# Twelve of twenty-two pairs per half by seven products in the down projection, with some activation sums kept, and fast pairs later in the gate's first half

## The chip, the cores and the metric

One Trainium2 chip, one of its cores. The metric is the device time in microseconds (us) of one execution of the whole program, as the median of three runs. A profile is one further execution, recorded instruction by instruction.

## The reference

One encoder layer on 256 tokens of width 2048, in float32. Cut to the parts that matter here (the mixer ahead of them yields `h`):

```python
hn = rmsnorm(h, ffn_norm_pre)
up = hn @ w_ffn_up                        # 2048 -> 2 x 5632
gate, val = split(up, 2)
gate = dwconv_centred(gate, ffn_conv_w, ffn_conv_b)
ff = (gelu(gate) * val) @ w_ffn_down      # "down": 5632 -> 2048
h = h + rmsnorm(ff, ffn_norm_post)
g = sigmoid(rmsnorm(h, ple_norm_pre) @ w_ple_gate)      # "gate": 2048 -> 2048
h = h + rmsnorm(g * (p @ w_ple), ple_norm_post)         # "PLE"
```

## The kernel before

**Precision and cost of a product.** Every float32 operand of a large product is split into a high and a low part of a type that TensorE reads at full speed (`split`, from line 139): ScalarE copies the high part (L150), VectorE subtracts it from the original for the low part (L151). A product is then three matmuls: high by high, high by low, low by high.

**Token-major products** (`token_major`, from line 289) compute down and gate. The output is 256 tokens by 2048 columns. It is made in two halves of 1024 columns; a half keeps four accumulators of 128 tokens by 512 columns in PSUM. The contraction runs in units `u` of two blocks of 128 (`k`, `k+1`): 22 units per half of down (5632 = 44 x 128), 8 per half of the gate. The order of the blocks comes from a list `ks`. A unit is done in one of two ways:

- *classic*: one load of 1 MB (`raw`, three buffers), two splits of 128 x 1024, 24 matmuls;
- *fast* (`seven_products`, when `u` is in the list `fast`): the unit is a product of two by two blocks (two token halves, two k blocks, two column halves) and is formed with seven block products instead of eight, 21 matmuls. It needs sums of weight blocks and sums of activation blocks. Four splits are made: `a` (128 x 512) and `b` (128 x 1024) of raw weight blocks (loads of 256 and 512 KB), `c` and `d` (128 x 1024) of the block sums `t` (1 MB). The products' order is: three matmuls with `a`, six with `b`, six with `c`, six with `d`. Some products go to extra accumulators `alt`, and `combine` adds them at the end of the half with VectorE.

**Sums of weight blocks** (`block_sums`) are formed ahead of time, during the up projection. Each is a fetch of two weight blocks into a page, three additions on VectorE, and a store to DRAM, put as jobs into a list `work` with 88 slots, of which `feature_pairs` runs one after each of its rounds; sum `i` uses the slots 3i+2 to 3i+5. The list `which` holds the pairs in order of use; its first two are formed last and stay in their pages, with no store. All others are loaded back when their unit needs them (`dns`, `gts` in the profile are the DRAM copies, `dn012t` is the load for half 0, k=12; as output of a matmul, `dns`, `dn0s`, `gts` and `gt0s` are the accumulators `alt`).

**Sums of activation blocks.** In down `hid_sums` (line 898) forms them from the page of activations at each fast unit, in both halves anew: four VectorE instructions of 128 x 128 into a `mid` tile `hd` (L757 to L760 in `pair_sums`), a ScalarE copy (L761) and a VectorE subtraction (L762) of 128 x 512 into a `mid` tile `he`. In the gate the class `Sums` does the same, with the result in half a page (`psp`), and keeps it: the second half finds the pairs of the first in `got`. `get_hid` splits the activations of a unit (`hs`, L883 and L884).

**Memory and order.** There are 13 pages of 128 x 2048 for large tiles (six hold the activations `hid` during down, others the output `dnm`, the residual `hb`, block sums, panels), three `mid` tiles, three raw buffers, five split buffers of each kind. Loads go out in order on one queue (SP). The framework places waits and orders each engine's instructions at build time; the program sets the priorities by its order. At unit 13 of down's second half the residual is loaded back (`back`), at unit 16 the gate's first pair is loaded and split ahead (`first_gate`: `gtf`, `gtfh`, `gtfl`).

After down, `panel_part` transposes the normalised result into the gate's stationary operand (`dnx`), PLE's product is formed, `row_rstd` squares the rows (junk in pages `rpj`), and the gate's two halves follow.

The lists that the change touches are on lines 845 and 846:

```python
dn_fast, gt_fast = ((2, 4, 6, 8, 9, 11, 13, 14, 16, 18, 19), (1, 3, 5, 7, 8, 10, 12, 14, 16, 17, 19)), ((2, 4, 6), (1, 2))
gt_ks = list(range(NK)), [0, 1, 4, 5, 8, 9, 2, 3, 6, 7, 10, 11, 12, 13, 14, 15]
```

Of the kernel before, what the change touches and what calls it, by code (L numbers as in the profile page):

```python
# [12 lines left out]
F32R = mybir.dt.float32r  # L13
# [3 lines left out]
P = 128  # L17
L = 256
D = 2048
NK = D // P  # L20
# [31 lines left out]
def build(nc, a, out):  # L52
# [5 lines left out]
    with tile.TileContext(nc) as tc, \  # L58
# [12 lines left out]
        def page(name, dtype=F32):  # L71
            return gp.tile([P, 2048], dtype, tag="pg", bufs=13, name=name)

        def mid(name, dtype=F32):
            return gp.tile([P, 1024], dtype, tag="mid", bufs=3, name=name)
# [365 lines left out]
        for u in range(0, NK, 2):  # L441
            r = [wp.tile([P, 2048], F32, tag="raw", bufs=3, name=f"dtur{u}") if u else r0, page(f"dtur{u + 1}")]
            for j in range(2):
                k = u + j
# [17 lines left out]
            for j in range(2):  # L462
                k = u + j
# [290 lines left out]
        def pair_sums(name, s, o, a11, a21, a12, a22):  # L754

            s1, s2, s3, s4 = (s[:, i * P:(i + 1) * P] for i in range(4))
            nc.vector.tensor_sub(s1, a22, a21)  # L757
            nc.vector.tensor_sub(s3, a11, a21)
            nc.vector.tensor_add(s2, s1, a11)
            nc.vector.tensor_sub(s4, a12, s2)  # L760
            nc.scalar.copy(o[:, :512], s[:, :512])  # L761
            nc.vector.tensor_sub(o[:, 512:], s[:, :512], o[:, :512].bitcast(F32))  # L762
            return {f"s{i + 1}": (o[:, i * P:(i + 1) * P], o[:, 512 + i * P:512 + (i + 1) * P]) for i in range(4)}
# [78 lines left out]
            h_kept.append(dp.tile([P, D], F32, tag=f"h{t}", bufs=1, name=f"h_kept{t}"))  # L842
            load(h_kept[t], h[t])

        dn_fast, gt_fast = ((2, 4, 6, 8, 9, 11, 13, 14, 16, 18, 19), (1, 3, 5, 7, 8, 10, 12, 14, 16, 17, 19)), ((2, 4, 6), (1, 2))
        gt_ks = list(range(NK)), [0, 1, 4, 5, 8, 9, 2, 3, 6, 7, 10, 11, 12, 13, 14, 15]
        which = [("dn", w_down, c * 1024, 2 * u) for c in range(2) for u in dn_fast[c]] + \
            [("gt", w_gate, c * 1024, gt_ks[c][2 * u]) for c in range(2) for u in gt_fast[c]]
        work.extend([] for _ in range(8 * DFF // 512))
# [3 lines left out]
        hid = []  # L853
        for s in range(DFF // 512):
            sc = mid(f"gr{s}")
            for i in range(2):
                ga = main(f"ga{s}{i}")
                feature_pairs(f"ug{s}{i}", w_up, s * 512 + i * 256, hf, ga)
                o = sc[:, i * 512:(i + 1) * 512]
# [7 lines left out]
            for i in range(2):  # L867
# [5 lines left out]
                hd = hid[s // 2][:, c0:c0 + 512]  # L873
# [5 lines left out]
        def get_hid(k):  # L879
            if k % 2 == 0:  # L880
                t = lp.tile([P, 1024], F32R, tag="hs", bufs=2, name=f"hs{k}")
                src = hid[k // 8][:, (k % 8) * L:(k % 8 + 2) * L]
                nc.scalar.copy(t[:, :512], src)  # L883
                nc.vector.tensor_sub(t[:, 512:], src, t[:, :512].bitcast(F32))  # L884
                cur["t"] = t
            o = (k % 2) * L
            return cur["t"][:, o:o + L], cur["t"][:, 512 + o:512 + o + L]
# [3 lines left out]
        def hid_get(k):  # L891
# [3 lines left out]
                hcache[k0], hcache[k0 + 1] = get_hid(k0), get_hid(k0 + 1)  # L895
            return hcache[k]

        def hid_sums(k):

            (h1, l1), (h2, l2) = get_hid(k), get_hid(k + 1)  # L900
            src = hid[k // 8][:, (k % 8) * L:(k % 8 + 2) * L]
            d = pair_sums(f"hd{k}", mid(f"hd{k}"), mid(f"he{k}", F32R), *(src[:, i * P:(i + 1) * P] for i in range(4)))
            return dict(d, a11=(h1[:, :P], l1[:, :P]), a12=(h2[:, :P], l2[:, :P]), a22=(h2[:, P:], l2[:, P:]))

        def back():
# [5 lines left out]
        def first_gate():  # L911
# [7 lines left out]
            for j in range(2):  # L919
                ready[f"gt00_{j}"] = hi[:, j * 1024:(j + 1) * 1024], lo[:, j * 1024:(j + 1) * 1024]  # L920

        hp = sublayer("dn", w_down, list(range(NF)), hid_get, gload("gffn", a["ffn_norm_post"][0]), h, V_PN,
                      fast=dn_fast, sums=hid_sums, at={13: back, 16: first_gate})


# [114 lines left out]
```

## Time and profile before

| | us |
|---|---|
| median of three runs | 1142.09 (1141.17 to 1142.82) |
| the profiled execution, its own time | 1140.26 |
| its span, first to last instruction | 1138.5 |
| TensorE busy | 1115.9 (98%) |
| VectorE busy | 935.8 (82%) |
| ScalarE busy | 637.6 (56%) |
| mean granted TensorE clock | 0.995 |

In the profile PE is TensorE's matmuls and PEld its weight loads, DVE is VectorE, ACT ScalarE, POOL GpSimd, SP the engine whose queue issues the DMAs. L87 is line 87 of the kernel. A row of a timeline gives start and duration in us, engine, line, operation, output and inputs by the program's names, shapes, and in brackets the idle time of the engine just before and what ended it. Matmuls overlap: a duration of 0.39 us goes with a start every 0.23 us, so starts are compared. A row of the table by stage gives the stage, its length, then for each engine the busy time and the number of instructions, then the granted clock, the share of time that the DMA engines were busy and their rate. A row of waits gives who waited for whom: us in total, times, the longest. A row of a DMA issue ends with KB and the us from issue to landing.

### The profile page before, as it was taken

The numbers are of one execution on the slowest core, as the hardware profiler recorded it, in microseconds if no ns is written. First come the engines' busy times: TensorE is split into PE (matmuls) and PEld (weight loads), VectorE is DVE, ScalarE is ACT, GpSimd is POOL, SyncE is SP. The second block draws the span as 40 slices with busy tenths as digits, with TensorE's granted clock in tenths as the row PEclk, the third lists the DMA queues.
The fourth block names the chain that finished last, engine by engine and source line by source line (L and its number), as shares of the span: only waits on it lengthen the run. The fifth ranks groups of instructions, "written<-read, shape, count | busy, mean of one in ns | idle before, by whom it ended". The sixth has DMA issues, their size and how long they took to land.

```text
span 1138.5 us, 15770 instructions
## 1 busy us (share of the span) xinstructions
PE 1115.9 (98%) x5982; PEld 962.5 (85%) x5982; DVE 935.8 (82%) x1277; ACT 637.6 (56%) x869; POOL 128.9 (11%) x124
## 2 busy tenths in 40 slices
PE   9998999999999999999999999999999999998996
PEld 9997987888888888888888888888888888886775
DVE  6579896699888877877877778867799999998795
ACT  7533543555674554544545545545677777776672
POOL 0274504200110100000000000000000000102001
PEclk9999999999999999999999999999999999999999
DMA  9952347545699999998999898966985589985673
GB/s 359 341 184 75 112 151 263 200 164 187 240 311 332 328 325 313 320 294 299 333 335 313 291 323 309 323 218 223 352 286 184 176 301 344 343 277 193 203 236 107
DMA packets 145419, 297.97 MB, mean 262 GB/s; under 512 B 5440, under 2 KB 98496, under 8 KB 137536
## 3 DMA queue, kind: packets, MB, share of 16 engines
q1 hardware_dynamic: 144784, 295.56, 76.4%
q0 software_dynamic: 272, 1.05, 0.5%
q8 instruction: 47, 0.77, 0.3%
q10 hardware_dynamic: 288, 0.36, 0.1%
q14 instruction: 28, 0.23, 0.1%
HBM read 266.54 MB, written 30.41 MB: 261 GB/s over the span
## 4 chain that ended last, share of the span: by engine, by line
PE 91%; DVE 5%; ACT 1%; DMA 1%; POOL 1%; issue 1%; DVEq 0%; POOLq 0%; ACTq 0%
PE va L87 22%; PE ga L87 21%; PE dna L87 15%; PE woa L87 7%; PE gt L87 4%; PE dtu L87 4%; PE z L87 4%; PE xbc L87 3%; PE dns L87 3%; DVE cv L426 2%; PE dn0s L87 1%; PE dn1s L87 1%; PE ple L87 1%; DMA gt04t<-gts 1%; DVE w L639 1%
## 5 line engine op out<-in xcount | busy, mean ns | idle before, releaser
L87 PE MATMUL ga<-wox,ug_0h 128*128 128x512 f32 x352 | 125.6, 395 | 0.0
L87 PE MATMUL ga<-wox,ug_1h 128*128 128x512 f32 x352 | 125.1, 394 | 0.0
L87 PE MATMUL va<-wox,uv_1h 128*128 128x512 f32 x352 | 124.8, 394 | 0.0
L87 PE MATMUL va<-wox,uv_0h 128*128 128x512 f32 x352 | 124.8, 394 | 0.0
L87 PE MATMUL ga<-wox,ug_1l 128*128 128x256 f32 x352 | 99.3, 282 | 0.0
L87 PE MATMUL ga<-wox,ug_0l 128*128 128x256 f32 x352 | 99.3, 282 | 0.0
L87 PE MATMUL va<-wox,uv_1l 128*128 128x256 f32 x352 | 99.2, 282 | 0.0
L87 PE MATMUL va<-wox,uv_0l 128*128 128x256 f32 x352 | 99.2, 282 | 0.0
L87 PEld LDWEIGHTS va<-wox,uv_1h 128*128 128x128 f32 x352 | 66.2, 188 | 14.8
L87 PEld LDWEIGHTS va<-wox,uv_0h 128*128 128x128 f32 x352 | 66.2, 188 | 14.8
L87 PEld LDWEIGHTS ga<-wox,ug_0h 128*128 128x128 f32 x352 | 66.2, 188 | 14.7
L87 PEld LDWEIGHTS ga<-wox,ug_1h 128*128 128x128 f32 x352 | 66.2, 188 | 14.7
L865 POOL TENSOR_TENSOR fc<-fc,rfb 128x1024 f32<-128x1024 f32 x11 | 28.0, 2546 | 438.6 <-ACT fc L864 438.6
L87 PEld LDWEIGHTS ga<-wox,ug_0l 128*128 128x128 f32 x352 | 66.3, 188 | 0.1
L87 PEld LDWEIGHTS ga<-wox,ug_1l 128*128 128x128 f32 x352 | 66.3, 188 | 0.0
L87 PEld LDWEIGHTS va<-wox,uv_0l 128*128 128x128 f32 x352 | 66.3, 188 | 0.0
L87 PEld LDWEIGHTS va<-wox,uv_1l 128*128 128x128 f32 x352 | 66.3, 188 | 0.0
L87 PE MATMUL dna<-dn_0h,hs 128*128 128x512 f32 x176 | 54.8, 394 | 0.0
L87 PE MATMUL dna<-dn_1h,hs 128*128 128x512 f32 x176 | 54.6, 393 | 0.0
L233 DVE TENSOR_TENSOR dnb<-dnb 128x1024 f32<-128x1024 f32 x22 | 28.0, 1271 | 16.1 <-DMA dnb<-w_ffn_down 16.1
L87 PEld LDWEIGHTS dna<-dn_1h,hs 128*128 128x128 f32 x176 | 33.1, 188 | 7.7
L87 PEld LDWEIGHTS dna<-dn_0h,hs 128*128 128x128 f32 x176 | 33.0, 188 | 7.6
(1866 smaller groups left out, 3136.0 us busy)
## 6 DMA issues: line engine op xcount, KB each, us to landing
dnb<-w_ffn_down SPq DMA_DIRECT2D x22, 1024.0 KB, 10.2
dns<-dnb SPq DMA_DIRECT2D x20, 1024.0 KB, 7.3
dn0r<-w_ffn_down SPq DMA_DIRECT2D x11, 1024.0 KB, 5.8
dn1r<-w_ffn_down SPq DMA_DIRECT2D x11, 1024.0 KB, 7.4
zr<-w_in SPq DMA_DIRECT2D x8, 1024.0 KB, 5.1
dtur<-w_in SPq DMA_DIRECT2D x14, 528.0 KB, 8.8
wo0r<-w_out SPq DMA_DIRECT2D x7, 1024.0 KB, 5.5
wo1r<-w_out SPq DMA_DIRECT2D x6, 1024.0 KB, 5.7
```

Of the source, the lines that this page charges most:

```text
L87: nc.tensor.matmul(o, lhsT, rhs, start=start, stop=stop, skip_group_check=True)
L233: nc.vector.tensor_add(v[:, 0:2], v[:, 0:2], v[:, 1::2])
L426: nc.vector.scalar_tensor_tensor(o[:, lo:hi], i[:, lo + d:hi + d], vec(wcol + j * wstep + f), o[:, lo:hi], op0=ALU.mult, op1=ALU.add)
L639: nc.vector.scalar_tensor_tensor(w[:, h * P:(h + 1) * P], cbm[:, 0, g, t, :], dt[:, t, 8 * g + h:8 * g + h + 1], w[:, h * P:(h + 1) * P], ...
L865: nc.gpsimd.tensor_tensor(cv.rearrange("p (f t) -> p f t", f=4), cv.rearrange("p (f t) -> p f t", f=4), rfb.unsqueeze(1).to_broadcast([P, ...
```

## The change

Three lists and one function are changed:

- down's fast units become 2, 3, 5, 7, 8, 10, 12, 13, 15, 16, 18, 19 in both halves: twelve instead of eleven, and the same ones in both;
- the activation sums of units 3, 8, 13 and 18 (k = 6, 16, 26, 36) are written by the first half not into a `mid` tile but into half a page each (two pages, `hsum6` and `hsum26`), kept, and used again by the second half without forming them;
- the gate's first half has fast units 4 and 6 (k = 8, 12) instead of 2, 4 and 6 (k = 4, 8, 12). Its second half keeps fast units 1 and 2, and its order of blocks is changed so that these are k = 12 and 8 instead of 4 and 8, whose activation sums the first half has formed. 28 sums of weight blocks are formed in place of 27; the two that stay in pages are those of down's units 2 and 3 instead of 2 and 4.

```diff
-        dn_fast, gt_fast = ((2, 4, 6, 8, 9, 11, 13, 14, 16, 18, 19), (1, 3, 5, 7, 8, 10, 12, 14, 16, 17, 19)), ((2, 4, 6), (1, 2))
-        gt_ks = list(range(NK)), [0, 1, 4, 5, 8, 9, 2, 3, 6, 7, 10, 11, 12, 13, 14, 15]
+        dn_fast, gt_fast, dn_keep = ((2, 3, 5, 7, 8, 10, 12, 13, 15, 16, 18, 19), (2, 3, 5, 7, 8, 10, 12, 13, 15, 16, 18, 19)), ((4, 6), (1, 2)), (3, 8, 13, 18)
+        gt_ks = list(range(NK)), [0, 1, 12, 13, 8, 9, 2, 3, 4, 5, 6, 7, 10, 11, 14, 15]
...
+        keep, kept = [], {}
+
         def hid_sums(k):

             (h1, l1), (h2, l2) = get_hid(k), get_hid(k + 1)
-            src = hid[k // 8][:, (k % 8) * L:(k % 8 + 2) * L]
-            d = pair_sums(f"hd{k}", mid(f"hd{k}"), mid(f"he{k}", F32R), *(src[:, i * P:(i + 1) * P] for i in range(4)))
+            if k not in kept:
+                src = hid[k // 8][:, (k % 8) * L:(k % 8 + 2) * L]
+                n = dn_keep.index(k // 2) if k // 2 in dn_keep else -1
+                if n >= 0 and n % 2 == 0:
+                    keep.append(page(f"hsum{k}", F32R))
+                o = keep[-1][:, n % 2 * 1024:(n % 2 + 1) * 1024] if n >= 0 else mid(f"he{k}", F32R)
+                d = pair_sums(f"hd{k}", mid(f"hd{k}"), o, *(src[:, i * P:(i + 1) * P] for i in range(4)))
+                if n >= 0:
+                    kept[k] = d
+            else:
+                d = kept[k]
             return dict(d, a11=(h1[:, :P], l1[:, :P]), a12=(h2[:, :P], l2[:, :P]), a22=(h2[:, P:], l2[:, P:]))
```

## The prediction

> **What bounds the kernel now.** I read the table of busy time by stage first, then the list of what TensorE waited for, then the chain of waits, and last the single instructions around the one long wait. The stages are: up projection to 798 us, first half of down to 912, second half to 1027, then PLE and gate.
>
> ```profile
> core 0: us, PE busy (x) PEld busy (x) DVE busy (x) ACT busy (x) POOL busy (x), PEclk, DMA share, GB/s
> 302.00:798.00 496.00, 495.45 (x2848) 435.45 (x2847) 396.19 (x509) 257.30 (x345) 29.48 (x15) 1.00 0.92 304
> 798.00:912.00 114.00, 114.00 (x496) 92.79 (x495) 102.64 (x144) 79.29 (x106) 0.00 (x0) 1.00 0.72 246
> 912.00:1027.00 115.00, 115.00 (x500) 93.50 (x499) 107.82 (x156) 85.12 (x110) 4.87 (x7) 1.00 0.90 313
> 1027.00:1060.00 33.00, 28.26 (x129) 21.88 (x128) 29.08 (x54) 22.49 (x39) 5.20 (x10) 0.95 0.59 212
> ```
>
> TensorE is busy without a gap in both halves of down and all but 0.55 us of up. There, only fewer matmuls shorten the time. VectorE is close behind (102.64 of 114, 107.82 of 115), so it is the engine to watch when work is added. Only at 1027 to 1060 does TensorE stand still, for 4.7 us, and its clock falls to 0.95. The list of its waits says why:
>
> ```profile
> PE gts L87 <- ACT gt04ch L150: 3.4, 1, 3.4
> PE gts L87 <- DVE gt04cl L151: 0.5, 1, 0.5
> ```
>
> Both belong to the pair k=4 of the gate's first half, its third pair and first by seven products. Its matmuls, and the first of the classic pair behind it:
>
> ```profile
> 1048.03 0.39 PE L87 MATMUL gts<-gt04ah,dnxh 128*128 128x512 f32 x1
> ...
> 1056.48 0.63 PE L87 MATMUL gt0s<-gt04cl,psp 128*128 128x512 f32 x1
> 1056.91 0.63 PE L87 MATMUL gt0s<-gt04ch,psp 128*128 128x512 f32 x1
> ...
> 1059.23 0.62 PE L87 MATMUL gt<-gt_0h,dnxh 128*128 128x512 f32 x2
> ```
>
> The pair took 1059.23 - 1048.03 = 11.20 us. What such a pair costs undisturbed is in the chain of waits, from down:
>
> ```profile
> 845.31 0.69 PE dns L87 x3
> ...
> 850.18 5.55 PE dna L87 x24
> 855.73 0.69 PE dns L87 x3
> ```
>
> From 845.31 to 850.18 runs a pair by seven products (21 matmuls): 4.87 us. The classic pair (24 matmuls) takes 5.55, so a fast pair saves 0.69 (three matmuls at 0.231). Hence the gate's first fast pair loses 11.20 - 4.87 = 6.33 us: the 3.9 us of waiting, and matmuls afterwards at a pitch of 0.43 instead of 0.23 us. The cause is in the DMA queue's own order and the line of DMA load (1030 to 1100, 1.75 us a digit):
>
> ```profile
> 1044.55 0.38 SPq L119 DMA_DIRECT2D gt0r<-w_ple_gate  x1
> 1045.02 0.42 SPq L119 DMA_DIRECT2D gt04t<-gts  x1
> 1045.49 0.42 SPq L119 DMA_DIRECT2D gt08t<-gts  x1
> 1049.08 0.32 SPq L119 DMA_DIRECT2D gt012t<-gts  x1
> ```
>
> ```profile
> DMA  9500059008999993078950399920398999903968
> ...
> gt08t<-gts SPq DMA_DIRECT2D x1, 1024.0 KB, 10.1
> ```
>
> The block sums gt04t are asked for at 1045.02, three microseconds before the pair begins, although the DMA engines stood nearly idle from 1033.5 to 1038.7 and from 1042.3 to 1045.7 (the digits 0). They stand in the queue behind weight loads that wait for raw buffers, and behind pages (13 in all) that the panel, the junk of the row sums and the activation sums ask for first. It is too late a start, not too little bandwidth.
>
> **The gate, part by part.** The fast pairs of its first half become those at units 4 and 6 (k=8, 12) instead of 2, 4 and 6. One classic pair replaces a fast one: +0.69. Units 2 and 3, both classic, now cover the loads: they need only raw weights, which go out ahead of these loads in the queue, and one load of 1 MB each in place of three. If they start at 1048.03 as the third unit does now, unit 4 starts at 1048.03 + 2 x 5.55 = 1059.1, and its first product from block sums nine matmuls later, at 1061.2. The block sums then still have to be split:
>
> ```profile
> 1053.11 1.04 ACT L150 CAST gt04ch<-gt04t 128x1024 fp32r<-128x1024 f32 x1 [2.50 <-DMA gt04t<-gts]
> ```
>
> ```profile
> 1054.19 1.23 DVE L151 TENSOR_TENSOR gt04cl<-gt04t,gt04ch 128x1024 fp32r<-128x1024 f32 x1 [2.69 <-ACT gt04ch L150]
> ```
>
> That is 1055.42 - 1053.11 = 2.3 us, so they must land by 1058.9. The very same load, gt08t, is issued at 1045.49 and takes 10.1 us: it lands at 1055.6, 3.3 us early. It has one load of 1 MB less ahead of it now, and the sums for k=4 with their page go away. So I cost the wait at nothing, and the 6.33 us go: -6.33 + 0.69 = -5.64. If the cover fails, each microsecond beyond 3.3 comes back. The second half keeps two fast pairs in the same places (k=12, 8 for 4, 8, the cached sums again): zero.
>
> **Down, part by part.** Eleven fast pairs per half become twelve: 2 x 0.69 = -1.39, on an engine without gaps, if nothing else gets late. VectorE's price, by starts of neighbouring instructions:
>
> ```profile
> 834.09 0.68 DVE L151 TENSOR_TENSOR dn016al<-dn016r,dn016ah 128x512 fp32r<-128x512 f32 x1
> 834.69 1.22 DVE L151 TENSOR_TENSOR dn016bl<-dn016r,dn016bh 128x1024 fp32r<-128x1024 f32 x1
> 835.83 0.68 DVE L884 TENSOR_TENSOR hs<-hid,hs 128x512 fp32r<-128x512 f32 x1
> 836.43 1.22 DVE L151 TENSOR_TENSOR dn016cl<-dn016t,dn016ch 128x1024 fp32r<-128x1024 f32 x1
> 837.56 0.69 DVE L762 TENSOR_TENSOR he<-hd,he 128x512 fp32r<-128x512 f32 x1
> 838.28 0.29 DVE L757 TENSOR_TENSOR hd<-hid 128x128 f32<-128x128 f32 x1
> 838.49 0.28 DVE L758 TENSOR_TENSOR hd<-hid 128x128 f32<-128x128 f32 x1
> ...
> 845.06 1.23 DVE L151 TENSOR_TENSOR dn018dl<-dn018t,dn018dh 128x1024 fp32r<-128x1024 f32 x1
> ```
>
> A 512-wide split 0.60, a 1024-wide one 1.14, the activation sums 4 x 0.21 + 0.72 = 1.55. A fast pair costs VectorE 0.60 + 3 x 1.14 + 0.60 + 1.55 = 6.17 against 4.87 of TensorE; a classic one 2 x 1.14 + 0.60 = 2.88 against 5.55. So the first half's load is 102.64 + 3.29 = 105.9 in about 113.3, the second's 107.82 + 3.29 - 4 x 1.55 = 104.9: it fits on average. Locally, the new order holds the run fast, fast, classic three times over (units 12 to 19). One round is 2 x 6.17 + 2.88 = 15.22 for VectorE, 2 x 4.87 + 5.55 = 15.29 for TensorE: even. What two fast pairs in a row leave of its lead is shown by dn018 (row above, done at 846.29) and its use:
>
> ```profile
> 848.85 0.40 PE L87 MATMUL dna<-dn018dl,hs 128*128 128x512 f32 x1
> ```
>
> That is 2.6 us, which a balanced round does not eat. In the second half the kept sums take another 1.55 off each round but the one at units 15 and 16. I cost VectorE at nothing; without that lead, a whole imbalance of 1.3 us per doubled pair would show, five per half.
>
> The kept sums themselves remove work from VectorE and ScalarE only, where TensorE does not wait: nothing by themselves, but they pay for the twelfth pair. Their two pages last into the second half and make block sums wait for pages. Behind such a load in the queue stand the weight loads of the following units.
>
> The DMA engines carry 0.79 MB more per half (768 KB of weights and 1024 KB of sums, against 1024 KB). In the second half, at 313 GB/s for 0.90 of the time, that is 0.79 MB / 348 GB/s = 2.3 us. Its tightest load now is dn138t:
>
> ```profile
> ACT dn138ch L150 <- DMA dn138t<-dns: 0.4, 1, 0.4
> ```
>
> ```profile
> 1008.84 1.22 DVE L151 TENSOR_TENSOR dn138cl<-dn138t,dn138ch 128x1024 fp32r<-128x1024 f32 x1
> ```
>
> ```profile
> 1013.06 0.39 PE L87 MATMUL dns<-dn138cl,he 128*128 128x512 f32 x1
> ```
>
> ScalarE waits for it, yet the split is done at 1010.06 and used at 1013.06: 3.0 us to spare. 2.3 us of it go, so the price lies between 0 and 2.3. I take 0.3, near the end that the spare time points to.
>
> **Up.** 28 block sums are formed instead of 27. The last one's addition falls some three slots before the stage's end, under a TensorE that is busy anyway and a VectorE at 396 of 496: nothing.
>
> **The sum.** -5.64 - 1.39 + 0.3 = -6.7 us on the profiled execution's 1140.26, so 1133.5 there; the median of the runs lies 1.83 higher, 1142.09, which gives 1135.4. About 0.2% (2.3 us) is what a measurement of this kernel tells from no change.
>
> **Rivals.**
> *A remainder of the gate's wait.* If the raw load ahead of the block sums is released later (it now waits for a classic pair's second split), gt08t could go out as late as gt012t does now, or later. At 1051, two microseconds after that, it would land at 1061.1 and TensorE would wait 2.2 us; at the old stall's ratio of 6.33 lost for 3.9 of waiting that costs 3.6: 1139.0. For it: the queue is in order. Against: the 3.3 us of margin. There is a rule on this price: by the Trainium skill, "TensorE: Matmul & The Clock Gate", Part 1, the clock is halved only after an idle window of about 3.4 us. The trace agrees, since the wait of 3.4 us was followed by the pitch of 0.43. By that rule a wait of 2.2 us would cost 2.2, and the time would be 1137.6.
>
> *The wait moves whole*, to unit 4 or into the classic pairs: 1135.4 + 6.3 = 1141.7, no change. Against: weights of units 2 and 3 are there early.
>
> *DMA late in the second half of down:* the full 2.3 us and once more as much for fewer pages: 1135.1 + 4.6 = 1139.7.
>
> *Slower: too few pages.* At the start of the second half six pages hold activations, two the output, one the PLE product and two the kept sums: two are left for block sums, and about unit 14, when the two pages of h and three of the gate's first weights are asked for, one. A page is held from issue to the last split:
>
> ```profile
> dn138t<-dns SPq DMA_DIRECT2D x1, 1024.0 KB, 11.5
> ```
>
> 11.5 us of landing and some 5 us to the last split, 16.5; with one page a fast pair is served every 16.5 us where a round of 15.29 wants two, one in 7.6; each waits 8.9 us, less the lead of 2.6. Two such waits cost 12.6: 1148. It decides if two fast pairs in a row find only one page. Against: activation pages come free at units 4, 8, 12 and 16.
>
> **How the numbers follow.** Forecast 0.62; a remainder 0.13; DMA late 0.09; moved whole 0.07; too few pages 0.09. The first three, 0.84, are faster by over 0.2% (below 1139.8); moved whole gives 0.07 within; the last 0.09 slower. The range goes from 1134.0 (the gate's other waits of under a microsecond gone too) to 1139.7, the end of the third case, which leaves 0.16 out above.
>
> **What the profile would show.** Right: no wait of TensorE for gt08c of over 0.5 us, the gate's clock at 1.00, both halves of down about 0.7 us shorter and without gaps, gt08t landing before unit 4. Wrong: gaps in down with ScalarE waiting for a dn..t load (pages or DMA), or splits on VectorE ending just ahead of their matmul in units 12 to 19 (VectorE's lead gone), or the wait for gt08c still there.

## The result, and the profile after

The changed kernel takes 1132.62 us in the median (four runs, 1132.56 to 1134.26), the kernel before 1141.63 (four runs, 1141.06 to 1142.82): a ratio of 0.9923, with an interval of 0.9911 to 0.9935, so 9.0 us less. The forecast was 1135.4, the low end of its range 1134.0: the sign and the places were right, the gain was larger than the range allowed. The profiled execution took 1134.26 us, 1.64 above its own median, while the profiled execution of before (1140.26) lay below nearly all of its timed runs. Between the two profiles lie only 6.0 us.

The table by stage of the profile after, in the windows shown of before (TensorE, its weight loads, VectorE, ScalarE, GpSimd, granted clock, DMA share, GB/s):

```profile
302.00:798.00 496.00, 495.44 (x2847) 434.60 (x2845) 402.28 (x519) 258.22 (x347) 29.50 (x15) 1.00 0.92 307
798.00:912.00 114.00, 114.00 (x498) 92.79 (x497) 105.43 (x146) 80.94 (x106) 0.00 (x0) 1.00 0.76 262
912.00:1027.00 115.00, 114.76 (x496) 92.61 (x496) 104.95 (x143) 84.86 (x110) 3.24 (x6) 1.00 0.91 322
1027.00:1060.00 33.00, 33.00 (x160) 26.88 (x159) 28.86 (x49) 23.14 (x40) 5.17 (x12) 1.00 0.65 214
```

The last row is the change's main effect: TensorE is busy for all 33.0 us instead of 28.26, at full clock instead of 0.95. VectorE's loads in down's halves, 105.43 and 104.95, are those that were worked out (105.9 and 104.9). The new order of the gate's loads in the DMA queue's timeline, the landing from the list of DMA issues, and the split and its use:

```profile
1043.40 0.38 SPq L119 DMA_DIRECT2D gt0r<-w_ple_gate  x1
1045.71 0.33 SPq L119 DMA_DIRECT2D gt08t<-gts  x1
1051.92 0.80 SPq L119 DMA_DIRECT2D gt012r<-w_ple_gate  x2
1052.77 0.42 SPq L119 DMA_DIRECT2D gt012t<-gts  x1
```

```profile
gt08t<-gts SPq DMA_DIRECT2D x1, 1024.0 KB, 6.5
```

```profile
1056.80 1.23 DVE L151 TENSOR_TENSOR gt08cl<-gt08t,gt08ch 128x1024 fp32r<-128x1024 f32 x1 [0.26 <-ACT gt08ch L150]
```

```profile
1061.01 0.39 PE L87 MATMUL gts<-gt08ch,psp 128*128 128x512 f32 x1
```

The block sums go out at 1045.71, as early as before, land 6.5 us later, are split by 1058.03 and used from 1061.01: three microseconds to spare, where TensorE waited 3.9 before. Units 2 and 3 cover the load, as forecast. What TensorE still waits for behind 302 us is this (the list of its waits; the first line belongs to the up projection and is there before too, 0.5 us), and the last line's matmul with its neighbour:

```profile
PE rfbp L87 <- DVE rfbw L401: 0.6, 1, 0.6
PE gt L87 <- DVE gt112bl L151: 0.4, 1, 0.4
PE dna L87 <- DVE hs L884: 0.2, 1, 0.2
```

```profile
1022.78 0.40 PE L87 MATMUL ple<-ple_0h,pth 128*128 128x512 f32 x1
1023.36 0.50 PE L87 MATMUL dna<-dn_0h,hs 128*128 128x512 f32 x1 [0.18 <-DVE hs L884]
```

### The profile page after: what moved, and what is told of

Its sections match the earlier page's. It is cut to its first block, busy times and chain, and to the rows that moved or that the text cites. A ratio compares the mean times of both kernels' runs of the same rounds, so it can differ in the third digit from the quotient of the medians.

```text
span 1132.4 us, 15774 instructions
## 1 busy us (share of the span) xinstructions
PE 1114.5 (98%) x5979; PEld 960.3 (85%) x5979; DVE 937.4 (83%) x1266; ACT 637.2 (56%) x868; POOL 127.3 (11%) x124
## 4 chain that ended last, share of the span: by engine, by line
PE 88%; DVE 6%; DMA 2%; ACT 2%; issue 1%; POOL 1%; SPq 0%; DVEq 0%; POOLq 0%; ACTq 0%
PE va L87 22%; PE ga L87 21%; PE dna L87 12%; PE woa L87 7%; PE gt L87 5%; PE z L87 4%; PE dtu L87 4%; PE xbc L87 3%; PE dns L87 2%; DVE cv L426 2%; PE dn0s L87 1%; DMA dn138t<-dns 1%; PE dn1s L87 1%; PE ple L87 1%; DMA dtur<-w_in 1%
## 5 line engine op out<-in xcount | busy, mean ns | idle before, releaser
L87 PE MATMUL dna<-dn_0h,hs 128*128 128x512 f32 x160 | 50.2, 394 | 0.2 <-DVE hs L884 0.2
L87 PE MATMUL dna<-dn_1h,hs 128*128 128x512 f32 x160 | 49.9, 393 | 0.0
L233 DVE TENSOR_TENSOR dnb<-dnb 128x1024 f32<-128x1024 f32 x24 | 30.3, 1261 | 13.6 <-DMA dnb<-w_ffn_down 13.5
L883 ACT CAST hs<-hid 128x512 fp32r<-128x512 f32 x44 | 27.1, 617 | 22.9 <-PE dna L87 18.3
L884 DVE TENSOR_TENSOR hs<-hid,hs 128x512 fp32r<-128x512 f32 x44 | 30.2, 687 | 9.7 <-ACT hs L883 9.7
## 6 DMA issues: line engine op xcount, KB each, us to landing
dnb<-w_ffn_down SPq DMA_DIRECT2D x24, 1024.0 KB, 10.2
```

Source lines behind the costliest of these rows:

```text
L87: nc.tensor.matmul(o, lhsT, rhs, start=start, stop=stop, skip_group_check=True)
L233: nc.vector.tensor_add(v[:, 0:2], v[:, 0:2], v[:, 1::2])
```

## The experiments

All were timed beside the kernel before, whose medians on the chips used were 1141.5 to 1142.1. To compare profiles stage by stage I took the starts of matmuls: the first `va` of the up stage (the matmuls ahead of it are the same in every kernel; from it to the first `dna` I call the up stage), the first and last `dna`, the first `gt`, and the end of the last `gt`. A matmul that does not follow within 0.231 us of the one before it counts as time lost.

| kernel | profiled, us | first `va` | down | gate | timed median, us | ratio (95%) |
|---|---|---|---|---|---|---|
| before | 1140.26 | 328.99 | 228.66 | 96.11 | 1141.63 | 1 |
| after | 1134.26 | 330.35 | 227.99 | 89.55 | 1132.62 | 0.9923 (0.9911 to 0.9935) |
| after again | 1132.93 | 329.66 | 227.54 | 89.52 | 1132.93 | 0.9922 (0.9910 to 0.9935) |
| gate's change alone | 1135.67 | 330.62 | 229.24 | 89.47 | 1134.62 | 0.9936 (0.9923 to 0.9950) |
| down's change alone | 1140.42 | 328.56 | 227.54 | 96.12 | 1141.09 | 0.9995 (0.9986 to 1.0004) |
| before again | 1140.92 | 329.17 | 229.04 | 96.21 | 1141.98 | 1.0001 (0.9992 to 1.0010) |

### The two parts alone, and both kernels again

Gate alone and down alone:

```diff
 # gate alone: the kernel before with
-((2, 4, 6), (1, 2))
+((4, 6), (1, 2))
-gt_ks = list(range(NK)), [0, 1, 4, 5, 8, 9, 2, 3, 6, 7, 10, 11, 12, 13, 14, 15]
+gt_ks = list(range(NK)), [0, 1, 12, 13, 8, 9, 2, 3, 4, 5, 6, 7, 10, 11, 14, 15]
 # down alone: the changed kernel with the old gate lists, 29 sums, and
-work[3 * i + 2 + j].extend(jobs)
+work[3 * i + j].extend(jobs)
```

> The changed kernel once more. It was 9.0 us faster by the medians, where the two profiled executions differ by 6.0 and, from the up projection on, by 7.3. Theory A (the gate's wait has a price that changes from run to run, since the TensorE clock falls after it; the profiled execution of before was a cheap one): 8 to 10 us faster again, and its own executions lie closer together than those of before. Theory B (chance of the two samples; the change is worth the 7.3 us of the profiles): 6.5 to 8 us.

> Only the gate's lists are changed (fast units 4 and 6 in its first half, the second half's order), down is as before. By the profiles the gate gave 7.3 of waits less 0.7 for one fast pair fewer: Theory B 6.6 us faster than before. Theory A: 7.5 to 9. Rival C (the gate's gain needs the change of down, which brings other waits before it): under 5.

> Only down is changed (twelve fast pairs per half, four sums kept); the gate has its old lists, so 29 block sums are formed, each two slots earlier in the up projection. Theories A and B: 1.39 less 0.8 of new waits in the second half, 0.6 us faster than before, with the gate's wait of 3.4 us there as before. Rival C: 3 us or more faster, or slower.

> The kernel before, timed against itself, for a second profile. Both: ratio 1.000 within 0.2%. Theory A: this profile shows more than 8.0 us lost by TensorE between 1027 and 1062 us (first profile 7.95), and the executions of before differ by over 1 us among themselves. Theory B: 8.0 again, and the difference sits ahead of 302 us.

The gate alone gives 7.1 us, down alone 0.6 (its interval includes no change), both 8.8. Theory C is out: neither part needs the other. The gate's stage is 6.6 us shorter in every kernel that has the new lists (96.11 to 96.21 against 89.47 to 89.55). Down's change seems worth only 0.6 us, but its kernel's up stage was 470.43 us long where all others so far have 469.04 or 469.05: the earlier slots cost 1.4 us there (the third group of experiments shows that it is the slots), and down's own stage gained 1.1 to 1.7. With those 1.4 us added back, the parts make up 9.1.

### Was the stall's price different in timed executions?

The timed runs of before are mostly at a mean granted clock of 0.992 (41 of the 51 that were timed beside the experiments, mean time 1141.9 us; the five at 0.995 have 1140.5), its profiles at 0.993 to 0.995. Kernels without the gate's stall have 0.994 to 0.997. So I took the stall away in two other ways, made it longer in a third, and profiled the kernel before twice more:

```diff
 # fast units 4, 5, 6 in the kernel before: as many matmuls, no early pair
-((2, 4, 6), (1, 2))
+((4, 5, 6), (1, 2))          # and gt_ks[1] as in the changed kernel
 # the lists of before, the first block sums asked for right after down
+early_t = page("gt04t")
+last["dma"] = load(early_t, sums_["gt", 0, 4][0], True)
+sums_["gt", 0, 4] = early_t, True
 # the first fast pair a unit earlier
-((2, 4, 6), (1, 2))
+((1, 4, 6), (1, 2))
+gt_ks = list(range(NK)), [0, 1, 2, 3, 8, 9, 4, 5, 6, 7, 10, 11, 12, 13, 14, 15]
```

> The kernel before with the gate's first half by fast units 4, 5, 6 instead of 2, 4, 6, and the second half's fast pairs k=12, 8: the same number of matmuls and the old down, only without the early block sums. Theory A (the stall costs 7.3 us in a cheap execution and 1 to 3 us more in most, since the clock falls after it): 8 to 9.5 us below the kernel before, and the single executions within 1.5 us of each other, at a granted clock of 0.994 or more. Theory B (the stall costs the 7.3 us of the profile in every execution): 7.3 us below, about 1134.4, and the executions spread by 3 us as those of the kernel before do.

> The kernel before, lists unchanged, with the load of the first gate pair's block sums (gt04t) asked for right after down, so that it stands in the queue ahead of the classic unit's weights that held it until 1045. It can go out at 1039, 6 us earlier, more than TensorE's 3.9 us of waiting: the stall goes, with no other change. By the prediction's account of the cause: 7.3 us less in the gate of the profile. Theory A (the stall costs more in timed executions than in profiled ones): the timed median falls by 8 to 9 us, to 1133 or 1134, at a clock of 0.994 or more. Theory B (its price is the profile's): by 7.3, to 1134.4. If a page and not the queue was the cause: no change, 1141.7.

> The kernel before with the gate's first fast pair at unit 1 (k=2) instead of 2, so 5.5 us earlier, while its block sums can go out no earlier than about 1045: TensorE waits about 4 + 5 = 9 us, partly filled by nothing. The timed median rises by 5.5 us to 1147, if each further us of waiting costs one; by more, up to 9 us, if the clock after it stays low for longer. Theory A: the offset between timed median and profile grows with the stall, and the mean clock falls below 0.992. Theory B: the offset stays.

> The kernel before, unchanged, for one more profile: most of its executions have a mean granted clock of 0.992 and 1141 to 1143 us, the profiled ones so far 0.993 to 0.995 and 1140.3 to 1140.9. Theory A (the price of the gate's stall changes): in an execution at 0.992, more than 8.0 us lost at 1027 to 1062, up to 1.7 us more, with a granted clock below 0.86 at 1048 to 1060. Theory B (the front part): the loss at 1027 to 1062 is 8.0 again, and the first matmul of the up stage's second kind comes later than 329.2, up to 331, after a lower clock at 100 to 150 (0.97 and 0.93 so far).

> The kernel before, unchanged, once more, for the same two theories: A, the loss at 1027 to 1062 grows with the time of the execution; B, the start of the up stage moves with it, and the loss at the gate stays 8.0.

Units 4, 5, 6: 1134.2 us, ratio 0.9934 (0.9921 to 0.9947), so 7.3 us less; its gate took 88.74 us in the profile, 7.4 less. The early load alone: 1135.45, ratio 0.9944 (0.9930 to 0.9957), 6.5 us less; its gate took 90.59. With the same matmuls in the same order as before, only this had moved (DMA queue's timeline):

```profile
1041.19 0.42 SPq L119 DMA_DIRECT2D gt04t<-gts  x1
1046.21 0.38 SPq L119 DMA_DIRECT2D gt0r<-w_ple_gate  x1
```

The load of the block sums now stands ahead of the weight load `gt0r`, which waits for a raw buffer, and goes out 3.8 us earlier than before, though this execution's gate began 2.0 us later. So the late load was the cause: the gate's stage is 5.6 us shorter in the profile without any other change, and 2.4 us are still lost at 1027 to 1062. Its place in the queue and the request for its page were moved together here; what each alone would do is open. The table by stage at 1048 to 1060, before, with the early load, and with the longer stall:

```profile
1048.00:1060.00 12.00, 7.83 (x25) 5.19 (x24) 9.21 (x14) 8.63 (x12) 1.73 (x4) 0.86 0.76 302
```

```profile
1048.00:1060.00 12.00, 11.72 (x49) 8.64 (x48) 11.39 (x19) 11.10 (x17) 2.20 (x6) 1.00 0.68 218
```

```profile
1048.00:1060.00 12.00, 8.46 (x20) 5.62 (x21) 10.66 (x16) 7.50 (x10) 0.11 (x1) 0.57 0.52 203
```

With the early load TensorE's waits here are at most 0.2 us and the clock stays at 1.00. The longer stall consists in the main of two waits with three matmuls between them (the second line is the earlier one, for the activation sums):

```profile
PE gts L87 <- ACT gt02ch L150: 3.4, 1, 3.4
PE gt L87 <- ACT psp L761: 3.0, 1, 3.0
```

After 3.4 us of waiting the clock of this window is 0.86, after 3.0 and 3.4 it is 0.57. The traces' record of the granted clock shows how this comes about. In all sixteen profiles the clock is 1.00 or 0.50, and it changes only on a grid of 3.41 us. Stretch by stretch of this grid, before (four rows) and with the longer stall (five rows); the second number of a row is the length, the third TensorE's busy time:

```profile
1048.17:1051.59 3.42, 2.40 (x9) 1.09 (x7) 3.23 (x8) 2.44 (x5) 1.73 (x4) 1.00 0.98 374
1051.59:1055.00 3.41, 0.73 (x2) 0.30 (x2) 0.81 (x1) 1.89 (x2) 0.00 (x0) 1.00 1.01 428
1055.00:1058.41 3.41, 2.94 (x7) 2.37 (x8) 3.41 (x4) 3.35 (x5) 0.00 (x0) 0.50 0.56 238
1058.41:1061.83 3.42, 3.42 (x16) 2.77 (x16) 3.33 (x4) 1.26 (x2) 0.00 (x0) 1.00 0.50 171
```

```profile
1045.35:1048.76 3.41, 0.65 (x2) 0.30 (x2) 1.67 (x5) 3.22 (x6) 1.11 (x4) 1.00 0.88 360
1048.76:1052.17 3.41, 0.87 (x2) 0.29 (x1) 2.32 (x8) 0.76 (x2) 0.00 (x0) 0.50 1.02 432
1052.17:1055.59 3.42, 2.53 (x5) 1.62 (x6) 3.17 (x4) 3.42 (x4) 0.00 (x0) 0.50 0.27 113
1055.59:1059.00 3.41, 3.41 (x9) 2.63 (x9) 3.41 (x4) 2.17 (x4) 0.00 (x0) 0.50 0.06 8
1059.00:1062.41 3.41, 3.41 (x16) 2.75 (x16) 1.51 (x2) 1.15 (x2) 0.00 (x0) 1.00 0.94 300
```

Half clock follows a stretch in which TensorE was hardly busy: 0.73 of 3.41 us before, 0.65 with the longer stall, there after a wait of only 3.0 us. Over the sixteen profiles, it followed every stretch with a busy share of at most 38% and none with 47% or more; full clock came back after a stretch at half clock with a share of at least 82%, and not after 81% or less (shares by the modelled ends of matmuls). So the price of a wait depends on where in the grid it falls. The Trainium skill, "TensorE: Matmul & The Clock Gate", Part 1, says that the clock halves after an idle window of about 3.4 us, and that the windows run on regardless of the kernel. The traces agree with the length, but the window need not be idle throughout.

The longer stall cost 2.9 us more than before in the timed runs (1144.86, ratio 1.0026, 1.0016 to 1.0036) and 4.3 in the gate's stage of its profile (100.42), where I had expected at least 5.5. The load went out at 1044.04, a microsecond earlier than before.

Theory A, that the stall costs more in most timed runs than in the first profile, is neither shown nor out. The longer stall's profile (1145.49) lies above its timed median, not below, at a clock of 0.990 to 0.994 in single runs, and the two further profiles of before, 1140.58 and 1141.28, lost 8.06 and 8.00 us at 1027 to 1062, as the first had lost 7.95. The price of the stall is the same in five profiles. But none of these is at the clock of 0.992 that most timed runs have. A mean of 0.992 stands for 17 to 19 us at half clock (an estimate from the rounded mean); the four profiles of before have 11.8 to 15.3, of which 3.41 at the gate, 3.41 or 6.83 shortly after 100 us and about 5 at the end. So most timed runs probably had one stretch at half clock more than any of these profiles. Since no timed run of a kernel without the stall is below 0.994, it probably lies at the stall, where it would cost up to 1.7 us, half its length; that is argued, not shown.

Something else differs between the profiles too. The clock at 100 to 150 us, first in the profile of before, then in that of 1141.28 us:

```profile
100.00:150.00 50.00, 46.35 (x332) 43.91 (x333) 42.81 (x81) 24.87 (x37) 18.48 (x12) 0.97 0.34 109
```

```profile
100.00:150.00 50.00, 46.71 (x331) 44.08 (x332) 42.23 (x80) 24.82 (x36) 18.48 (x12) 0.93 0.34 108
```

There TensorE has waited for 4.9 us, in every kernel alike, and the half clock at its end lasted one stretch of the grid in four of the sixteen profiles and two in twelve. The first `va` comes at 328.97 us in the mean of the four and at 329.67 in the mean of the twelve; but among the twelve alone it lies between 329.17 and 330.62, so the clock is only a part of this spread. And in down's second half, which I had read as free of gaps, only one of the two later profiles agrees with the first. Of the eight profiles with the old lists of down, two have no gap (1140.26 and 1140.58 us), six lose 0.4 to 0.9 us at about 1006. ScalarE's waits in the first profile, then those of the kernel with the early load, whose down is the same, and what TensorE waited for in it:

```profile
ACT dn_0h L150 <- DVE dn134dl L151: 0.8, 1, 0.8
```

```profile
ACT dn_0h L150 <- DMA dn1r<-w_ffn_down: 1.9, 1, 1.9
```

```profile
PE dna L87 <- DVE hs L884: 0.6, 1, 0.6
```

In most of the eight profiles the weights of a classic unit, `dn1r`, come up to two microseconds late, with the DMA engines busy nearly all the while (0.89 to 0.91 of 912 to 1027); VectorE's splits slip, and TensorE waits. The old down takes 228.66 to 229.59 us in eight profiles (mean 229.17), the new one 227.54 to 227.99 in six (mean 227.63). So down's change is worth 1.5 us in the profiles, not the 0.7 that the first two show.

### Do the kept activation sums pay?

Two of the four kept (units 3 and 8), and none:

```diff
-dn_keep = (3, 8, 13, 18)
+dn_keep = (3, 8)             # the other run: ()
```

> The changed kernel with only the activation sums of units 3 and 8 kept (one page instead of two); units 13 and 18 form theirs in both halves. If pages make down's second half late (its two small gaps, 0.45 to 0.78 us): those go, up to 0.8 us below the changed kernel, 1132.1 to 1132.9. If VectorE needs the relief of the kept sums: 2 x 1.55 us more work at units 13 and 18, where each can cost up to 1.3 us, so 1133.5 to 1135.5.

> The changed kernel with no activation sums kept: the second half of down forms all twelve anew. VectorE then has 104.8 + 4 x 1.55 = 111 us of work in a half of 114, TensorE's lead over it must carry three rounds of fast, fast, classic. By the prediction's account the kept sums pay for the twelfth pair: without them waits of TensorE for splits of 1 to 1.3 us at one to three places, 1134 to 1136.5. If VectorE's lead is enough (a round is 15.22 against 15.29): no wait, two pages more, 1132.2 to 1132.9.

With two kept 1133.78 us (ratio 0.9932, 0.9918 to 0.9946), with none 1134.80 (0.9939, 0.9926 to 0.9952), against 1132.93 and 0.9922 with four. Down took 228.62 and 229.53 us in the profiles, against 227.63: 1.0 and 1.9 us more. The gaps are waits for VectorE (none kept):

```profile
PE dna L87 <- DVE hs L884: 0.5, 1, 0.5
PE dns L87 <- DVE dn132cl L151: 0.2, 1, 0.2
```

Each is one profile, and the intervals of the three ratios overlap; but the order is the same in both measures. Without the kept sums the twelfth pair gives back about all that it brings. The rival, that their two pages make loads late, finds no support: with fewer pages held the kernel was not faster.

### A third fast pair in the gate's first half, and a later one in its second

```diff
 # 4, 5, 6 with slots two earlier; the same with the old first slots
-((4, 6), (1, 2))
+((4, 5, 6), (1, 2))
-work[3 * i + 2 + j]
+work[3 * i + j]              # the second run: 3 * i + 2 - max(0, i - 26) + j
 # the third run, besides
-((4, 5, 6), (1, 2))
+((4, 5, 6), (2, 3))
+gt_ks = list(range(NK)), [0, 1, 2, 3, 12, 13, 8, 9, 4, 5, 6, 7, 10, 11, 14, 15]
-for i in (8, 10):
+for i in (10,):
-token_major(f"gt{half}", w_gate, half * 1024, ks, hp, acc, 1 + 3 * half, fast, alt, hps)
+token_major(f"gt{half}", w_gate, half * 1024, ks, hp, acc, 1 + 2 * half, fast, alt, hps)
```

> The changed kernel with one more pair by seven products in the gate's first half (units 4, 5, 6 instead of 4, 6; 29 sums of weight blocks, formed in slots that begin two earlier). The cover theory (units 2 and 3 hide the loads, and bandwidth is not short): three matmuls fewer, so 0.69 us below the changed kernel's 1132.93, about 1132.2, if VectorE's lead lasts over three fast units in a row (3 x 1.3 us beyond their TensorE time, from two classic units that give it 2 x 2.7). Rival, the queue: the sums of unit 5 come 5 us after those of unit 4 in a queue in order; a late one makes TensorE wait 1 to 3 us, so 1133.5 to 1136.

> The changed kernel with gate fast units 4, 5, 6 and 29 sums, whose first slots are those of the changed kernel (the last two sums two slots apart instead of three). The profile of the version with slots two earlier showed the gate 0.7 us shorter and the up stage 1.3 us longer. If the early slots made that wait in up: up back at 469.05, gate 88.85, so 0.69 below the changed kernel, about 1132.2. If the 29th sum costs up its 1.3 us wherever it lies: about 1133.5.

> As the run before it, and the gate's second half with its fast pairs at units 2 and 3 instead of 1 and 2, the last three units instead of four drained together. The changed kernel's only wait of TensorE in the gate (0.4 us for gt112bl, 0.6 with the pitch behind it) comes since VectorE still evicts the first half then. If that is all: 0.6 us less, about 1131.6. Rival: with three units drained together instead of four the accumulators' evictions overlap less with the last matmuls, and the tail grows by 1 to 2 us: 1132.5 to 1134.

The first took 1134.10 us (ratio 0.9933, 0.9919 to 0.9947), the second 1132.92 (0.9921, 0.9907 to 0.9934), the third 1133.47 (0.9925, 0.9912 to 0.9937): none is told apart from the changed kernel as faster. In the first the gate is 88.85 us, 0.7 shorter as counted, and the up stage 470.33, 1.3 longer. Its wait, in TensorE's and ScalarE's timelines:

```profile
379.92 0.50 PE L87 MATMUL va<-wox,uv_0h 128*128 128x512 f32 x1
381.18 0.39 PE L87 MATMUL va<-wox,uv_0l 128*128 128x256 f32 x1 [0.76 <-DVE uv_0l L151]
```

```profile
378.82 1.05 ACT L150 CAST uv_0h<-uv10r 128x1024 fp32r<-128x1024 f32 x1 [4.05 <-DMA uv10r<-w_ffn_up]
```

The sums' loads and stores come two slots earlier and make the stage's own weights late. With the old first slots the up stage is back at 469.04 and the gate at 88.85, yet the timed median stays where it was: from the last matmul to the end the profile has 9.65 us instead of 8.93. The third run's gate is 88.13, its wait for VectorE gone, and the end 10.55 us behind the last matmul. The matmuls were saved, and the end did not move with them. The last VectorE work of the second run starts 0.92 us before that of the changed kernel (first row: the changed kernel again, second row: the second run), and so do the stores of the output behind it, which take 2.8 us to land in the median of both. What then holds the end is left open:

```profile
1124.61 2.74 DVE L967 SCALAR_TENSOR_TENSOR vg<-vg,go1r,hb 128x512 f32<-128x512 f32 x4 [0.81 <-POOL go1r L962]
```

```profile
1123.69 2.74 DVE L967 SCALAR_TENSOR_TENSOR vg<-vg,go1r,hb 128x512 f32<-128x512 f32 x4 [0.81 <-POOL go1r L962]
```

## Why the prediction was right or wrong, point by point

- **The gate's cover**: right. Units 2 and 3 hide the load, and the wait is gone. That the late load was the cause is shown by the early load alone.
- **The gate's size**: the step that failed. The mechanism was right, but the term was too small: 5.64 forecast, 6.64 measured (mean of five profiles with the old stage, 96.17, less 89.53, the mean of five with the new), and perhaps more in the timed runs. I read the price of the wait from the third unit alone, 6.33 us, and from one profiled execution. The stage lost 7.95 us, of which some 0.6 remain after the change; the largest piece that I missed is a pair's matmul, pulled ahead, behind which TensorE waited for ScalarE to move PLE's product out (before, TensorE's timeline):

```profile
1040.49 0.40 PE L87 MATMUL gt<-gt04bh,dnxh 128*128 128x512 f32 x1
1041.46 0.53 PE L87 MATMUL gt<-gtfh,dnxh 128*128 128x512 f32 x1 [0.58 <-ACT pl L822]
```

  Some 0.87 us are lost at these two matmuls. They are gone where the second and the third unit are both classic (at most 0.16 in the same place), and stay with the early load, whose pair is still the third.
- **Down**: 1.39 less 0.3 forecast, 1.5 measured over many profiles, 0.7 between the first two. The saving of 1.39 is as counted. The DMA term, +0.3, was wrong: the old order already lost 0.4 to 0.9 us at about 1006 in six of eight profiles (0.49 in the mean of all), and the new one loses 0.3 (five of six profiles) to 0.8 us (0.40 in the mean), so the term came out at -0.1. That both halves were without a gap was read from one execution, one of the two best of eight.
- **VectorE, the kept sums, pages, up**: right. VectorE's loads came out within 0.5 us, each pair of kept sums is worth about a microsecond in the profiles, no wait of TensorE for too few pages came up, and 28 sums left up at 469.04. "Without gaps" was not quite right for down, as said.
- **The price of a shorter wait**, a rival that did not come about: whether 2.2 us of waiting would have left the clock alone is open. Such a wait within one stretch of the grid leaves TensorE busy for about 36% of it, and stretches with up to 38% were followed by half clock.
- **From the profile to the median**: I added 1.83 us, the distance of one profiled execution to the median. That is the same as taking the sum of 6.7 off the median of 1142.09, and it takes for granted that the stages gain as much in a timed run as in that one profile. For the changed kernel the distance was -1.64 in its first profile and nil in its second. That 1133.5, the sum for the profiled execution, came within 0.8 of the measured 1134.26 is in part luck: that execution's first `va` came 1.36 us later than in the profile before.
- **What is explained**: gate 6.64 and down 1.5 make 8.2 of the 8.8 to 9.0 us; the rest lies within the interval (7.4 to 10.2). The 2.8 us by which the forecast lies above the median are thus 1.0 of the gate's term, 0.4 to 0.5 of down's, 0.5 of the base (the median of before is 1141.63 with a fourth run, not 1142.09), and 0.8 that no stage of a profile shows. The two terms alone would have put the forecast at the low end of its range, 1134.0. The timed runs of before lie about 0.9 us above the mean of its four profiles (1140.76), those of the stall-free kernels half a microsecond below theirs. One more stretch at half clock in most timed runs of before could account for the first of these; where it lies, no view of a timed run shows.

## What to carry to other kernels

Read a stall's price from the whole stage's lost pitch, not from the one unit where the long wait stands: small waits of the same order of work go with it. Take the absence of gaps, and the distance between profile and median, from several profiles, since each is one draw, and put the spread of the runs into the range. Compare the mean clock of the timed runs with that of the profile: where they differ, the profile may not show the common case. A load that is late although the DMA engines stand idle can be a matter of its place in an ordered queue; here either more work ahead of its use or an earlier request cured it.

## What the runs showed of the hardware

The granted clock was 1.00 or 0.50 and changed on a grid of 3.41 us in all sixteen profiles. A stretch with TensorE busy for at most 38% was followed by half clock, one with 47% or more was not, and full clock came back only after at least 82%. So the same 4.9 us wait was followed by 3.41 us of half clock in four profiles and by 6.83 in twelve (a mean clock of 0.97 or 0.93 at 100 to 150 us). A load of 1 MB, `gt08t`, issued at nearly the same time took 10.1 us to land in the one kernel and 6.5 in the other, with one load of 1 MB fewer ahead of it.
